# A decoder layer on one core: key tiles of 128, 128 and 16, and the order of attention and convolution work set by a VectorE budget

## The chip, the cores and the metric

The kernel runs on 1 core of one Trainium2 chip. The metric is the device time of one execution in microseconds (us); lower is better. The engines that matter here are TensorE (PE in the profile; PEld is its weight load), VectorE (DVE), ScalarE (ACT), GpSimd (POOL) and the queue that starts the weight transfers (SP).

## The reference, cut to what matters

One layer of a hybrid decoder, in float32: 16 meta tokens and 256 tokens (272 in all), model width 2048. One input projection feeds three groups of heads: 6 forgetting-attention heads ("fox"), 4 differential-attention heads ("diff") and a convolution module of 768 channels. Their outputs are joined, projected by `w_out`, added to the residual, and followed by a gated feed-forward part of width 5632.

```
h = rmsnorm(x);  proj = h @ w_in
fox : s = (q k^T) * 128**-0.5 + c[query] - c[key], causal;  p = softmax(s);  y = p @ v      # c = cumsum(log f)
diff: p = softmax(q1 k1^T / 8) - lam * softmax(q2 k2^T / 8), causal;  y = rmsnorm(p @ v) * 0.8
conv: u = a * sigmoid(g);  u = causal_dwconv31(u) + b;  y = silu(layernorm(u))
h = h + rmsnorm(concat(fox, diff, conv) @ w_out)
f = (silu(causal_dwconv3(h' @ w_gate)) * (h' @ w_up)) @ w_down        # h' = rmsnorm(h)
out = (h + rmsnorm(f))[16:]
```

The queries come in blocks: the 16 meta tokens, then 128 and 128 real tokens. A block sees all keys up to its own end. The kernel computes only the last two meta rows (258 query columns, `NQ`), since the later width-3 convolution needs no more of them.

## The kernel before, in words

Activations are kept transposed (features on partitions, tokens in the free dimension). Every projection multiplies a weight tile of 128x128 with 258 or 272 token columns. To keep float32 accuracy, both operands are cut into a high and a low part in fp32r, and `mm3` (L278 to L281) issues three matmuls: high by high, high by low, low by high. A weight chunk arrives by DMA on the SP queue (`load`), ScalarE makes its high part (L203), VectorE its low part (L204); `chunk()` does this one chunk ahead of its use.

**The input projection** runs in groups of up to four weight tiles (`in_groups`, `TOGETHER`); the text writes g4c2 for chunk 2 of group 4. Each chunk holds four k steps; after the fourth chunk `evac` copies the finished tiles out of PSUM. Group 1 and groups 4 and 5 give the convolution's inputs, groups 0, 2 and 3 the diff heads' q, k and v, groups 6 to 10 the fox heads'.

**Attention and convolution are laid between these matmuls by hand.** Each head is a Python generator (`fox`, L544; `diff`, L566). At a `yield` it stops until it is pumped again. In every chunk the first three heads that are waiting are pumped one stage each, after 8, 12 and 16 of the chunk's (tile, k) steps (L659). A fox head has the stages: scores and softmax; (empty); transposes of the probabilities (`probsT`); output. A diff head: scores and two softmaxes; their combination; (empty); transposes; output; (empty); normalised output. Behind the heads `pump_conv` (L256) issues convolution taps (L448, 31 taps for each of 6 channel tiles, 186 in all, VectorE) until a budget is spent: 2.1 or 1.9 a chunk, with 0.66 charged for two taps, 5.0 in group 10. When the taps are done, the same queue holds `layernorm` (L452), which goes through four stops: the sum over channel tiles; a matmul with ones (L459), subtractions and squares; the reciprocal root through TensorE, VectorE and GpSimd (`token_rstd`, L130, L120, L121); its spread over the partitions (L141) and the six results y10 to y15 (L478, L479, L486, L487). A bare `yield` there ends that pump.

**The output projection** (L685 to L714) works on four tiles at a time over 16 k steps in the order `KORD`: chunk 0 needs the diff heads' results y6 to y9, chunk 1 the fox heads' y0 to y3, chunk 2 y10 to y13 of the convolution, chunk 3 y14, y15, y4 and y5. Before each chunk of its first group the waiting heads and `pump_conv(4.0)` are pumped once (L688). The four PSUM banks of a group are held until its last chunk is done.

The compiler that turns the program into one instruction list for each engine keeps this order, except that an instruction whose inputs it takes to be late lets later ones go first.

**One head's tiles.** Keys are taken as 0 to 127 with only the first 16 counted (`vm`, scaled by a vector that is zero from 16 on), 16 to 143 and 144 to 271. `scores` (L508) makes 144 columns for the first block of queries, 272 for the second and 16 for the meta rows. `probsT` (L528) transposes six 128x128 pieces on TensorE into two PSUM banks; one VectorE copy (L538) and three ScalarE copies bring them back. The output takes three matmuls in a fox head (258, 256 and 128 columns) and six of 128 columns in a diff head. A float32 matmul is issued as two passes; a transpose is one. The masks are built by VectorE and GpSimd at the start (L103 to L112).

Of the kernel before, what the change touches and what calls it, by code (L numbers as in the profile page):

```python
# [9 lines left out]
F32 = mybir.dt.float32  # L10
# [7 lines left out]
P = 128  # L18
# [53 lines left out]
def hymba_kernel(ctx, tc, ins, out):  # L72
# [15 lines left out]
    def planes(n):  # L88
# [12 lines left out]
    mhalf = const.tile([P, 4], F32, name="mhalf")  # L101
# [15 lines left out]
    def rsqrt(out_t, in_t, n, d, eps, w):  # L117
        v = const.tile([P, 4], F32, name=f"var{cnt[0]}", tag="var", bufs=4)
# [213 lines left out]
    r0 = const.tile([P, 4], F32, name="r0")  # L332
    R0 = const.tile([P, T], F32, name="R0")
    r0f = const.tile([P, 4], F32, name="r0f")
    r0d = const.tile([P, 4], F32, name="r0d")
    r0m = const.tile([P, 1], F32, name="r0m")
    nc.vector.memset(r0m, 0.0)
# [33 lines left out]
    wf = const.tile([P, KT, FOXH], F32, name="wf")  # L371
# [65 lines left out]
    def conv(i):  # L437

        acc[i] = slot("C", NQ)
        for n, k in enumerate(range(CW - 1, -1, -1)):  # L440
# [8 lines left out]
            if n % 2:  # L449
                yield 0.66  # L450
# [42 lines left out]
    def values(vT, key):  # L493
        ps = bank()
        nc.tensor.transpose(out=ps[:, 0:P], in_=vT[:, 0:P], identity=ident)
        nc.tensor.transpose(out=ps[:, P:2 * P], in_=vT[:, NM:NM + P], identity=ident)
        nc.tensor.transpose(out=ps[:, 2 * P:3 * P], in_=vT[:, NM + P:T], identity=ident)
        v, vm = slot("T", 2 * P), slot("T", P)
        nc.scalar.mul(out=vm, in_=ps[:, 0:P], mul=r0m)
        nc.scalar.mul(out=v[:, 0:P], in_=ps[:, P:2 * P], mul=r0[:, 0:1])  # L500
        nc.scalar.mul(out=v[:, P:2 * P], in_=ps[:, 2 * P:3 * P], mul=r0[:, 1:2])
        return vm, v[:, 0:P], v[:, P:2 * P]

    def scores(maps):
# [3 lines left out]
        for o, n, a in ((0, 144, 2), (144, T, 130), (416, NM, 0)):  # L508
# [4 lines left out]
    def softmax_rows(ps, biasA, biasB, biasM, rs, key):  # L513

        pA, pB = slot("T", 160), slot("T", T)
        segs = ((pA[:, NM:160], ps[:, 0:144], biasA, P, 0), (pB, ps[:, 144:416], biasB, P, 1), (pA[:, 0:NM], ps[:, 416:432], biasM, P, 2))
# [9 lines left out]
        return [(pA[:, NM:160], P, 0), (pB, P, 1), (pA[:, 0:NM], P, 2)], pA, sm  # L526

    def probsT(pr, pA, key):  # L528
        pa, pb, pm = (x[0] for x in pr)
        tA, tB = bank(), bank()  # L530
        nc.tensor.transpose(out=tA[:, 0:P], in_=pa[:, 0:P], identity=ident)
        nc.tensor.transpose(out=tA[:, P:2 * P], in_=pb[:, 0:P], identity=ident)
        nc.tensor.transpose(out=tA[:, 2 * P:3 * P], in_=pa[:, 16:144], identity=ident)
        nc.tensor.transpose(out=tA[:, 3 * P:4 * P], in_=pb[:, 16:144], identity=ident)
        nc.tensor.transpose(out=tB[:, 0:P], in_=pb[:, 144:272], identity=ident)
        nc.tensor.transpose(out=tB[:, P:2 * P], in_=pA[:, 0:P], identity=ident)
        ptm, pta, ptb = slot("T", NQ), slot("T", 2 * P), slot("T", P)
# [443 lines left out]
```

## Time and profile before

| | |
|---|---|
| three runs | 1157.0, 1156.12, 1155.02 us; median 1156.12 |
| profiled execution | 1155.95 us, of which the span is 1154.1 us |
| PE busy | 1143.1 us (99%), 7768 matmuls |
| DVE busy | 765.4 us (66%) |
| ACT busy | 580.2 us (50%) |
| POOL busy | 69.4 us (6%) |
| granted TensorE clock | 0.998 of full speed |

Busy times are shares of the span. Matmuls overlap in their pipeline, so a matmul's own duration (some 0.28 us for 258 columns) is longer than the distance from its start to the next start (0.12 us); the distance is what it costs. VectorE's share is a mean over stages that differ: it is full in most of the input projection and at about half in the feed-forward part.

### The profile page before, as it was taken

What the parts mean: (1) busy time and instruction counts of PE and PEld (TensorE: products, weight loads), DVE (VectorE), ACT (ScalarE), POOL (GpSimd) and SP (SyncE); (2) the same over time, 40 slices, a digit from 0 to 9 for tenths busy, and PEclk for the clock granted to TensorE, in tenths of its full rate; (3) what the DMA queues carried; (4) which work ended last, traced back from release to release, by engine and by line L of the source; (5) the groups of instructions that cost most, each with busy time, mean ns of one, the idle gap of its engine ahead of it and who ended that gap; (6) DMA issues with size and microseconds to landing.
All of it is one profiled execution on the core that took longest, in us unless ns stands there. A gap on an engine that the chain in (4) does not pass through costs nothing.

```text
span 1154.1 us, 19333 instructions
## 1 busy us (share of the span) xinstructions
PE 1143.1 (99%) x7768; PEld 1059.2 (92%) x7768; DVE 765.4 (66%) x1298; ACT 580.2 (50%) x998; POOL 69.4 (6%) x120
## 2 busy tenths in 40 slices
PE   9999999999999999999999999999999999999997
PEld 8999999999999999999999999999999888888885
DVE  7699899985647589656766576567666645444544
ACT  8445764555856546544544454445445434343432
POOL 0010000001200038100000000000000100000001
PEclk9999999999999999999999999999999999999999
DMA  8555335333757437555555555555455755555554
GB/s 319 205 165 198 134 124 183 146 129 122 263 183 249 153 126 231 193 183 183 183 183 185 185 181 187 183 185 191 178 191 187 229 182 185 195 196 190 182 184 145
DMA packets 36522, 213.39 MB, mean 185 GB/s; under 512 B 5338, under 2 KB 8032, under 8 KB 12880
## 3 DMA queue, kind: packets, MB, share of 16 engines
q1 hardware_dynamic: 32400, 205.33, 49.6%
q0 software_dynamic: 3600, 6.29, 2.2%
q8 instruction: 61, 1.00, 0.3%
q10 hardware_dynamic: 432, 0.53, 0.2%
q14 instruction: 29, 0.24, 0.1%
HBM read 207.93 MB, written 4.20 MB: 184 GB/s over the span
## 4 chain that ended last, share of the span: by engine, by line
PE 97%; DMA 2%; DVE 1%; ACT 0%; issue 0%; SPq 0%; DVEq 0%; ACTq 0%
PE m L279 16%; PE m L280 16%; PE m L281 16%; PE m L774 13%; PE m L775 7%; PE m L854 4%; PE a L854 4%; PE m L856 4%; PE a L856 4%; PE a L855 4%; PE m L855 4%; DMA raw<-in_w_in 1%; PE a L774 1%; PE a L510 1%; PE a L281 1%; PE a L775 0%
## 5 line engine op out<-in xcount | busy, mean ns | idle before, releaser
L204 DVE TENSOR_TENSOR lo<-raw,hi 128x1024 fp32r<-128x1024 f32 (+2 forms) x382 | 452.0, 1202 | 320.6 <-ACT hi L203 319.4
L203 ACT CAST hi<-raw 128x1024 fp32r<-128x1024 f32 (+2 forms) x382 | 384.9, 1033 | 359.7 <-PE m L280 142.4
L279 PE MATMUL m<-R,hi 128*128 128x258 f32 (+1 forms) x1296 | 371.7, 288 | 1.1 <-ACT R L736 0.7
L280 PE MATMUL m<-R,hi 128*128 128x258 f32 (+1 forms) x1296 | 369.7, 286 | 0.0
L281 PE MATMUL m<-R,lo 128*128 128x258 f32 (+1 forms) x1296 | 368.0, 285 | 0.0
L279 PEld LDWEIGHTS m<-R,hi 128*128 128x128 f32 x1296 | 243.8, 189 | 3.2 <-ACT R L736 1.0
L280 PEld LDWEIGHTS m<-R,hi 128*128 128x128 f32 x1296 | 245.9, 190 | 0.3 <-DVE R L298 0.2
L281 PEld LDWEIGHTS m<-R,lo 128*128 128x128 f32 x1296 | 245.6, 190 | 0.0
L774 PE MATMUL m<-R,hi 128*128 128x512 f32 x656 | 231.2, 396 | 0.0
L775 PE MATMUL m<-R,lo 128*128 128x256 f32 x656 | 183.7, 280 | 0.0
L774 PEld LDWEIGHTS m<-R,hi 128*128 128x128 f32 x656 | 123.2, 188 | 27.9
L775 PEld LDWEIGHTS m<-R,lo 128*128 128x128 f32 x656 | 125.4, 191 | 0.0
L448 DVE SCALAR_TENSOR_TENSOR C<-C,vec,C 128x258 f32<-128x258 f32 (+12 forms) x180 | 80.6, 475 | 1.5
L279 PE MATMUL m<-Y,hi 128*128 128x258 f32 x256 | 72.9, 285 | 0.0
L280 PE MATMUL m<-Y,hi 128*128 128x258 f32 x256 | 72.6, 284 | 0.0
L281 PE MATMUL m<-Y,lo 128*128 128x258 f32 x256 | 72.0, 282 | 0.0
L280 PEld LDWEIGHTS m<-Y,hi 128*128 128x128 f32 x256 | 48.9, 191 | 0.0
L281 PEld LDWEIGHTS m<-Y,lo 128*128 128x128 f32 x256 | 48.8, 191 | 0.0
L279 PEld LDWEIGHTS m<-Y,hi 128*128 128x128 f32 x256 | 48.3, 189 | 0.0
L754 POOL DMA_DIRECT2D h1d<-K x64 | 37.1, 586 | 35.1 <-DVE K L752 29.8
L843 POOL DMA_DIRECT2D X<-in_gpost x8 | 4.4, 545 | 438.2 <-DVE T L796 427.5
L856 PE MATMUL m<-hi,Y 128*128 128x512 f32 x64 | 25.3, 395 | 0.0
(399 smaller groups left out, 1428.6 us busy)
## 6 DMA issues: line engine op xcount, KB each, us to landing
raw<-in_w_gate SPq DMA_DIRECT2D x44, 1024.0 KB, 4.8
raw<-in_w_down SPq DMA_DIRECT2D x44, 1024.0 KB, 4.8
raw<-in_w_up SPq DMA_DIRECT2D x41, 1024.0 KB, 4.8
raw<-in_w_in SPq DMA_DIRECT2D x37, 1024.0 KB, 4.8
raw<-in_w_out SPq DMA_DIRECT2D x16, 1024.0 KB, 5.1
raw<-in_w_in SPq DMA_DIRECT2D x8, 512.0 KB, 4.9
raw<-in_w_up SPq DMA_DIRECT2D x4, 768.0 KB, 4.2
X<-in_xT SPq DMA_DIRECT2D x16, 136.0 KB, 5.7
```

The costliest lines, as they stand in the source:

```text
L203: i = nc.scalar.copy(out=hi, in_=r)
L204: j = nc.vector.tensor_tensor(out=lo, in0=r, in1=hi.bitcast(F32), op=ALU.subtract)
L279: nc.tensor.matmul(out=ps, lhsT=wh, rhs=xh, start=first, stop=False)
L280: nc.tensor.matmul(out=ps, lhsT=wh, rhs=xl, start=False, stop=False)
L281: nc.tensor.matmul(out=ps, lhsT=wl, rhs=xh, start=False, stop=last)
L448: nc.vector.scalar_tensor_tensor(out=acc[i][:, j:NQ], in0=src, scalar=w, in1=acc[i][:, j:NQ], op0=ALU.mult, op1=ALU.add)
L754: nc.gpsimd.dma_start(out=place[j, i], in_=hs[32 * i:32 * i + 32, :].rearrange("a (q b) -> a q b", b=32))
L774: nc.tensor.matmul(out=both, lhsT=wh, rhs=hb[k][:, :, 2:NQ], start=k == 0, stop=False, skip_group_check=True)
L775: nc.tensor.matmul(out=ps[ti][:, 0:SEQ], lhsT=wl, rhs=hh[k][:, 2:NQ], start=False, stop=k == KT - 1, skip_group_check=True)
L854: nc.tensor.matmul(out=po[n][t], lhsT=ah[k][:, s], rhs=wh, start=k == 0, stop=False)
L855: nc.tensor.matmul(out=po[n][t], lhsT=ah[k][:, s], rhs=wl, start=False, stop=False)
L856: nc.tensor.matmul(out=po[n][t], lhsT=al[k][:, s], rhs=wh, start=False, stop=k == FT - 1)
```

## The change

The keys are taken as 0 to 127, 128 to 255 and 256 to 271 (all of the first tile counts). The score blocks get 160, 272 and 32 columns, the further ones masked, so that 32x32 squares line up. `probsT` makes three TensorE transposes into one bank; the three corners that these leave out are turned by VectorE in 32x32 squares. The targets `p0`, `e1`, `e2` are three standing sets whose unused parts `prepare` sets to zero once. A fox head's output takes 258, 144 and 16 columns. The values' tiles are scaled by the reciprocal roots of tokens 0, 128 and 144 on (`r0e` is zero below row 112), for which `stats0` computes a fifth window.

Masks are no longer built at the start but by GpSimd in `prepare`, called in g3c0. `wf` moves to a rotating buffer, and `R0` and `R2s` share one.

The empty stages go. Each `yield` now tells what the next stage costs; `pick` takes the waiting heads, in order, that fit a budget of 3.5 a chunk (less a charge for the copies of a chunk 3; the first is always taken), and the rest of the budget, at least 0.8, goes to convolution taps, two for 0.8. `CB` and its 5.0 in group 10 go.

```diff
-    mask = const.tile([P, 416], F32, name="mask")
-    nc.vector.memset(mask, 0.0)
-    nc.gpsimd.affine_select(out=mask[:, 0:144], in_=mask[:, 0:144], pattern=[[-1, 144]], base=NM,
-                            channel_multiplier=1, compare_op=ALU.is_ge, fill=NEG)
-    nc.gpsimd.affine_select(out=mask[:, 144:416], in_=mask[:, 144:416], pattern=[[-1, 272]], base=NM + P,
-                            channel_multiplier=1, compare_op=ALU.is_ge, fill=NEG)
-    maskm = const.tile([P, NM], F32, name="maskm")
-    nc.vector.memset(maskm, 0.0)
-    nc.gpsimd.affine_select(out=maskm, in_=maskm, pattern=[[-1, NM]], base=Q0,
-                            channel_multiplier=1, compare_op=ALU.is_ge, fill=NEG)
+    from112 = const.tile([P, 1], F32, name="from112")
+    nc.gpsimd.affine_select(out=from112, in_=ones[:, 0:1], pattern=[[0, 1]], base=-112, channel_multiplier=1, compare_op=ALU.is_ge, fill=0.0)
...
+    ahead = {}
+
     def pump_job(j):
         try:
-            next(j)
+            ahead[j] = next(j) or 0.0
         except StopIteration:
             heads.remove(j)
+
+    def pick(budget):
+
+        jobs = []
+        for j in list(heads)[:3]:
+            c = ahead.get(j, 1.0)
+            if c <= budget or not jobs:
+                jobs.append(j)
+                budget -= c
+        return jobs, budget
...
-        spread0 = token_rstd([ssx], float(D), EPS, (NM, NM + P, 0, Q0), ((2, 0, NM, 0), (0, 0, P, NM), (1, 0, P, NM + P)), r0, True, "m")
+        spread0 = token_rstd([ssx], float(D), EPS, (NM, NM + P, 0, Q0, P), ((2, 0, NM, 0), (0, 0, P, NM), (1, 0, P, NM + P)), r0, True, "m")
         yield
         ps = spread0(True)
         nc.scalar.copy(out=R0, in_=ps[:, 0:T])
-        nc.vector.tensor_copy(out=r0m[0:NM], in_=r0[0:NM, 2:3])
-        nc.vector.tensor_scalar(out=r0f, in0=r0, scalar1=FOXS, scalar2=None, op0=ALU.mult)
-        nc.vector.tensor_scalar(out=r0d, in0=r0, scalar1=DIFFS, scalar2=None, op0=ALU.mult)
+        nc.vector.tensor_tensor(out=r0e, in0=r0[:, 1:2], in1=from112, op=ALU.mult)
...
-                yield 0.66
+                yield 0.8
...
+    mask, sets, nset = [], [], [0]
+
+    def prepare():
+
+
+        ma, mb = slot("X", 192), slot("X", T)
+        for t, o, n, base in ((ma, 0, 160, NM), (ma, 160, 32, Q0), (mb, 0, T, NM + P)):
+            x = t[:, o:o + n]
+            nc.gpsimd.memset(x, 0.0)
+            nc.gpsimd.affine_select(out=x, in_=x, pattern=[[-1, n]], base=base, channel_multiplier=1, compare_op=ALU.is_ge, fill=NEG)
+        mask.extend([ma[:, 0:160], mb, ma[:, 160:192]])
+        for _ in range(3):
+            p0, e1, e2 = slot("X", NQ), slot("X", 256), slot("X", P)
+            for x in (p0[:, 0:2], e1[:, 0:P], e2):
+                nc.gpsimd.memset(x, 0.0)
+            sets.append((p0, e1, e2))
...
+        for i, (o, r) in enumerate(((0, r0[:, 2:3]), (P, r0[:, 4:5]), (NM + P, r0e))):
+            nc.tensor.transpose(out=ps[:, i * P:(i + 1) * P], in_=vT[:, o:o + P], identity=ident)
+            nc.scalar.mul(out=v[i], in_=ps[:, i * P:(i + 1) * P], mul=r)
+        return v
...
-        for o, n, a in ((0, 144, 2), (144, T, 130), (416, NM, 0)):
+        for o, n, a in ((0, 160, 2), (160, T, 130), (432, 32, 0)):
...
-    def probsT(pr, pA, key):
-        pa, pb, pm = (x[0] for x in pr)
-        tA, tB = bank(), bank()
-        nc.tensor.transpose(out=tA[:, 0:P], in_=pa[:, 0:P], identity=ident)
-        nc.tensor.transpose(out=tA[:, P:2 * P], in_=pb[:, 0:P], identity=ident)
-        nc.tensor.transpose(out=tA[:, 2 * P:3 * P], in_=pa[:, 16:144], identity=ident)
-        nc.tensor.transpose(out=tA[:, 3 * P:4 * P], in_=pb[:, 16:144], identity=ident)
-        nc.tensor.transpose(out=tB[:, 0:P], in_=pb[:, 144:272], identity=ident)
-        nc.tensor.transpose(out=tB[:, P:2 * P], in_=pA[:, 0:P], identity=ident)
-        ptm, pta, ptb = slot("T", NQ), slot("T", 2 * P), slot("T", P)
-        nc.vector.tensor_copy(out=ptm[:, 0:2], in_=tB[:, P:P + 2])
-        nc.scalar.copy(out=ptm[:, 2:NQ], in_=tA[:, 0:2 * P])
-        nc.scalar.copy(out=pta, in_=tA[:, 2 * P:4 * P])
-        nc.scalar.copy(out=ptb, in_=tB[:, 0:P])
-        return ptm, pta, ptb
+        return [(pA[:, 32:192], P, 0), (pB, P, 1), (pA[:, 0:32], P, 2)], (pA, pB), sm
+
+    def probsT(p):
+
+
+        pA, pB = p
+        p0, e1, e2 = sets[nset[0] % 3]
+        nset[0] += 1
+        ps = bank()
+        for i, x in enumerate((pA[:, 32:160], pB[:, 0:P], pB[:, P:256])):
+            nc.tensor.transpose(out=ps[:, i * P:(i + 1) * P], in_=x, identity=ident)
+        nc.vector.transpose(out=p0[0:32, 0:32], in_=pA[0:32, 0:32])
+        nc.vector.transpose(out=e1[0:32, 96:P], in_=pA[96:P, 160:192])
+        nc.vector.transpose(out=e2[96:P, 96:P], in_=pB[96:P, 240:T])
+        nc.scalar.copy(out=p0[:, 2:NQ], in_=ps[:, 0:256])
+        nc.scalar.copy(out=e1[:, P:256], in_=ps[:, 256:384])
+        return p0, e1, e2
...
             nc.scalar.mul(out=x, in_=x, mul=r[0:n, c:c + 1])
-        yield
-        if h < FOXH - 1:
-            yield
-        ptm, pta, ptb = probsT(p, pA, key)
-        yield
+        yield 0.6
+        p0, e1, e2 = probsT(pt)
+        yield 0.4
         o = bank()
-        nc.tensor.matmul(out=o[:, 0:NQ], lhsT=vm, rhs=ptm, start=True, stop=False)
-        nc.tensor.matmul(out=o[:, 2:NQ], lhsT=va, rhs=pta, start=False, stop=False)
-        nc.tensor.matmul(out=o[:, 130:NQ], lhsT=vb, rhs=ptb, start=False, stop=True)
+        nc.tensor.matmul(out=o[:, 0:NQ], lhsT=v[0], rhs=p0, start=True, stop=False)
+        nc.tensor.matmul(out=o[:, 114:NQ], lhsT=v[1], rhs=e1[:, 112:256], start=False, stop=False)
+        nc.tensor.matmul(out=o[:, 242:NQ], lhsT=v[2], rhs=e2[:, 112:P], start=False, stop=True)
...
     def diff(h, qT, kT, vT):
...
-        yield
+        yield 1.1
...
-        yield
-        yield
-        ptm, pta, ptb = probsT(p1, pA, key)
-        yield
+        yield 0.6
+        p0, e1, e2 = probsT(pt)
+        yield 0.2
...
-        yield
-        yield
+        yield 0.0
+        yield 0.4
...
-            heads.append(diff(i, q, k, v) if d else fox(i, q, k, v))
-
-    CB = {9: 2.1, 10: 5.0}
+            j = diff(i, q, k, v) if d else fox(i, q, k, v)
+            ahead[j] = 3.6 if d else 2.8
+            heads.append(j)
...
-                jobs = list(heads)[:3]
+                jobs, left = pick(3.5 - (sum(dict(k=0.4, a=0.6, g=0.6).get(x[0][-1], 0.0) for x in g) if c == 3 else 0.0))
...
                     lam()
+                    prepare()
...
-                    pump_conv(CB.get(gi, 2.1 if gi < 4 else 1.9))
+                    pump_conv(max(left, 0.8))
```

## Rows read from the trace of the kernel before

**Rows 1.** The page of the profile: busy us of each engine, share, instructions
```profile
PE 1143.1 (99%) x7768; PEld 1059.2 (92%) x7768; DVE 765.4 (66%) x1298; ACT 580.2 (50%) x998; POOL 69.4 (6%) x120
```

**Rows 2.** Waits of PE: engine, line, released by, us in total, times, longest
```profile
PE m L279 <- DVE C L431: 0.3, 1, 0.3
```

**Rows 3.** Windows: stretch, its length, busy PE, PEld, DVE, ACT, POOL (instructions), clock, DMA
```profile
108.00:140.00 32.00, 32.00 (x267) 31.20 (x266) 25.20 (x75) 25.37 (x76) 0.00 (x0) 1.00 0.39 141
...
246.00:279.00 33.00, 33.00 (x261) 32.57 (x260) 16.44 (x38) 17.97 (x47) 0.00 (x0) 1.00 0.25 90
279.00:294.60 15.60, 15.60 (x126) 15.35 (x125) 14.17 (x36) 12.71 (x31) 5.17 (x7) 1.00 0.78 277
```

**Rows 4.** Timeline of PE, one head's transposes: start, us, engine, line, operation
```profile
210.81 0.27 PE L531 MATMUL a<-ident,T 128*128 128x128 f32 x1
...
211.35 0.27 PE L536 MATMUL a<-ident,T 128*128 128x128 f32 x1
```

**Rows 5.** Timeline of PE, one fox head's output
```profile
217.36 0.60 PE L561 MATMUL a<-T,T 128*128 128x258 f32 x2
217.80 0.59 PE L562 MATMUL a<-T,T 128*128 128x256 f32 x2
218.23 0.38 PE L563 MATMUL a<-T,T 128*128 128x128 f32 x2
```

**Rows 6.** Timeline of PE, one fox head's scores (first rows, last pass, next matmul)
```profile
199.28 0.41 PE L510 MATMUL a<-Q,Q 128*128 128x144 f32 x2
...
200.01 0.26 PE L510 MATMUL a<-Q,Q 128*128 128x16 f32 x1
200.12 0.36 PE L279 MATMUL m<-R,hi 128*128 128x258 f32 x1
```

**Rows 7.** Timeline of all engines, the layer norm's steps
```profile
278.05 0.60 PE L459 MATMUL a<-C,ones 128*128 128x258 f32 x2
...
286.33 0.80 PE L130 MATMUL a<-ones,C 128*128 128x1 f32 x6
...
287.98 1.89 POOL L121 TENSOR_TENSOR rt<-var,mhalf 128x3 f32<-128x3 f32 x1
...
289.95 0.80 PE L141 MATMUL a<-ident,rt 128*128 128x128 f32 x6
...
290.90 2.08 DVE L478 TENSOR_TENSOR C<-C,a 128x258 f32<-128x258 f32 x6
...
291.40 1.05 ACT L203 CAST hi<-raw 128x1024 fp32r<-128x1024 f32 x1
292.47 1.28 ACT L479 ACT_TABLE_LOAD   x1
...
293.76 1.10 ACT L479 ACTIVATE C<-C,vec 128x258 f32<-128x258 f32 x2
...
297.60 0.43 DVE L487 TENSOR_TENSOR Y<-C,Y 128x258 fp32r<-128x258 f32 x1 [0.37 <-ACT Y L486]
```

**Rows 8.** Timeline of ACT: a table load whose activation waits for VectorE
```profile
64.20 1.28 ACT L360 ACT_TABLE_LOAD   x1
68.23 0.20 ACT L360 ACTIVATE lamex<-lamsm 128x2 f32<-128x2 f32 x1 [2.75 <-DVE lamsm L358]
```

**Rows 9.** Timeline of PE, the output projection's start and fox head 5's scores in it
```profile
294.63 0.37 PE L279 MATMUL m<-Y,hi 128*128 128x258 f32 x1
...
299.52 0.27 PE L495 MATMUL a<-ident,Q 128*128 128x128 f32 x1
...
300.69 0.36 PE L281 MATMUL m<-Y,lo 128*128 128x258 f32 x1
```

**Rows 10.** One line's instructions: the small VectorE copy (ns least, median, most)
```profile
L538 DVE COPY T<-a x10: 148/155/160, 133.4 to 309.6; 128x2 f32<-128x2 f32 x10
```

**Rows 11.** Windows at the end of the span, columns as in rows 3
```profile
1145.30:1149.90 4.60, 0.17 (x1) 0.00 (x0) 3.73 (x9) 1.68 (x6) 1.96 (x3) 1.00 0.48 161
1149.90:1154.00 4.10, 0.00 (x0) 0.00 (x0) 0.04 (x1) 0.00 (x0) 0.00 (x0) 0.50 0.52 165
```

More of the change, by code (lines that the diff above doesn't have):

```diff
@@ L117, in rsqrt @@
     def rsqrt(out_t, in_t, n, d, eps, w):
-        v = const.tile([P, 4], F32, name=f"var{cnt[0]}", tag="var", bufs=4)
+        v = const.tile([P, 5], F32, name=f"var{cnt[0]}", tag="var", bufs=4)
         cnt[0] += 1
@@ L330, in hymba_kernel @@
     nc.vector.tensor_scalar(out=gs, in0=vec[:, V_GSUB:V_GSUB + 1], scalar1=1.0 - LAM_INIT, scalar2=None, op0=ALU.mult)
-    r0 = const.tile([P, 4], F32, name="r0")
-    R0 = const.tile([P, T], F32, name="R0")
+    r0 = const.tile([P, 5], F32, name="r0")
+    R0 = const.tile([P, T], F32, name="R0", tag="spread")
     r0f = const.tile([P, 4], F32, name="r0f")
     r0d = const.tile([P, 4], F32, name="r0d")
-    r0m = const.tile([P, 1], F32, name="r0m")
-    nc.vector.memset(r0m, 0.0)
+    r0e = const.tile([P, 1], F32, name="r0e")
     def stats0():
-        spread0 = token_rstd([ssx], float(D), EPS, (NM, NM + P, 0, Q0), ((2, 0, NM, 0), (0, 0, P, NM), (1, 0, P, NM + P)), r0, True, "m")
+        spread0 = token_rstd([ssx], float(D), EPS, (NM, NM + P, 0, Q0, P), ((2, 0, NM, 0), (0, 0, P, NM), (1, 0, P, NM + P)), r0, True, "m")
         yield
@@ L369, in hymba_kernel @@
     ckb, cqA, cqM = [], const.tile([P, 2, 6], F32, name="cqA"), const.tile([P, 6], F32, name="cqM")
-    wf = const.tile([P, KT, FOXH], F32, name="wf")
+    wf = slot("T", KT * FOXH).rearrange("p (k h) -> p k h", h=FOXH)
     nc.gpsimd.dma_start(out=wf, in_=ins["w_f"])
@@ L490, in put_y, with values @@
             nc.vector.scalar_tensor_tensor(out=yl[k], in0=src, scalar=scale, in1=yh[k].bitcast(F32), op0=ALU.mult, op1=ALU.subtract)
-    def values(vT, key):
-        ps = bank()
[L495 to L502, printed above, removed]
+    mask, sets, nset = [], [], [0]
[11 more added lines that the diff above has]
+            sets.append((p0, e1, e2))
+    def values(vT):
+        ps = bank()
+        v = slot("T", 2 * P), slot("T", P)
+        v = v[0][:, 0:P], v[0][:, P:2 * P], v[1]
+        for i, (o, r) in enumerate(((0, r0[:, 2:3]), (P, r0[:, 4:5]), (NM + P, r0e))):
+            nc.tensor.transpose(out=ps[:, i * P:(i + 1) * P], in_=vT[:, o:o + P], identity=ident)
+            nc.scalar.mul(out=v[i], in_=ps[:, i * P:(i + 1) * P], mul=r)
+        return v
     def scores(maps):
         pss = [bank() for _ in maps]
-        for o, n, a in ((0, 144, 2), (144, T, 130), (416, NM, 0)):
+        for o, n, a in ((0, 160, 2), (160, T, 130), (432, 32, 0)):
             for ps, (qT, kT) in zip(pss, maps):
@@ L544, in fox @@
     def fox(h, qT, kT, vT):
         key = f"f{h}"
-        vm, va, vb = values(vT, key)
-        biA, biB = slot("T", 144), slot("T", T)
-        biasm = wk.tile([P, NM], F32, tag="biasm", name=f"biasm{h}")
-        nc.vector.scalar_tensor_tensor(out=biA, in0=mask[:, 0:144], scalar=cqA[:, 0, h:h + 1], in1=ckb[h][:, 0:144], op0=ALU.add, op1=ALU.subtract)
-        nc.vector.scalar_tensor_tensor(out=biB, in0=mask[:, 144:416], scalar=cqA[:, 1, h:h + 1], in1=ckb[h], op0=ALU.add, op1=ALU.subtract)
-        nc.vector.scalar_tensor_tensor(out=biasm, in0=maskm, scalar=cqM[:, h:h + 1], in1=ckb[h][:, 0:NM], op0=ALU.add, op1=ALU.subtract)
@@ L552, in fox @@
-        p, pA, r = softmax_rows(scores([(qT, kT)])[0], biA, biB, biasm, r0f, key)
+        v = values(vT)
+        bi, biB = slot("T", 192), slot("T", T)
+        nc.vector.scalar_tensor_tensor(out=bi[:, 0:160], in0=mask[0], scalar=cqA[:, 0, h:h + 1], in1=ckb[h][:, 0:160], op0=ALU.add, op1=ALU.subtract)
+        nc.vector.scalar_tensor_tensor(out=biB, in0=mask[1], scalar=cqA[:, 1, h:h + 1], in1=ckb[h], op0=ALU.add, op1=ALU.subtract)
+        nc.vector.scalar_tensor_tensor(out=bi[:, 160:192], in0=mask[2], scalar=cqM[:, h:h + 1], in1=ckb[h][:, 0:32], op0=ALU.add, op1=ALU.subtract)
@@ L576, in diff @@
             nc.vector.scalar_tensor_tensor(out=x, in0=y, scalar=rb[0:n, c:c + 1], in1=x, op0=ALU.mult, op1=ALU.add)
-        yield
-        yield
-        ptm, pta, ptb = probsT(p1, pA, key)
-        yield
+        yield 0.6
+        p0, e1, e2 = probsT(pt)
+        yield 0.2
         o = bank()
-        nc.tensor.matmul(out=o[:, 0:P], lhsT=ptm[:, 2:130], rhs=vm, start=True, stop=False)
-        nc.tensor.matmul(out=o[:, 0:P], lhsT=pta[:, 0:P], rhs=va, start=False, stop=True)
-        nc.tensor.matmul(out=o[:, P:2 * P], lhsT=ptm[:, 130:258], rhs=vm, start=True, stop=False)
-        nc.tensor.matmul(out=o[:, P:2 * P], lhsT=pta[:, P:2 * P], rhs=va, start=False, stop=False)
-        nc.tensor.matmul(out=o[:, P:2 * P], lhsT=ptb, rhs=vb, start=False, stop=True)
-        nc.tensor.matmul(out=o[:, 2 * P:3 * P], lhsT=ptm[:, 0:P], rhs=vm, start=True, stop=True)
+        nc.tensor.matmul(out=o[:, 0:P], lhsT=p0[:, 2:130], rhs=v[0], start=True, stop=False)
+        nc.tensor.matmul(out=o[:, 0:P], lhsT=e1[:, 0:P], rhs=v[1], start=False, stop=True)
+        nc.tensor.matmul(out=o[:, P:2 * P], lhsT=p0[:, 130:258], rhs=v[0], start=True, stop=False)
+        nc.tensor.matmul(out=o[:, P:2 * P], lhsT=e1[:, P:256], rhs=v[1], start=False, stop=False)
+        nc.tensor.matmul(out=o[:, P:2 * P], lhsT=e2, rhs=v[2], start=False, stop=True)
+        nc.tensor.matmul(out=o[:, 2 * P:3 * P], lhsT=p0[:, 0:P], rhs=v[0], start=True, stop=True)
         ss = wk.tile([P, 3], F32, tag="ss", name=f"ss{h}")
@@ L729, in hymba_kernel @@
     h1d = dpool.tile([SEQ, D], F32, name="h1d")
-    R2s = const.tile([P, NQ], F32, name="R2s")
+    R2s = const.tile([P, NQ], F32, name="R2s", tag="spread")
     def h1(j):
```

16 lines of the change are left out of this document (9 added, 7 removed).

## The prediction, made before the change was run

> **What bounds the kernel now.** I read the page's busy times first. TensorE is busy 99% of the span, VectorE 66%, ScalarE 50% [rows 1]. The waits of TensorE come next: of four waits in the whole span one lies among the attention work, 0.3 us for VectorE's gate copies [rows 2]. So the kernel takes what TensorE's instruction stream takes, and a change pays by taking instructions out of that stream or costs by putting a hole into it. The windows tell where VectorE could make such a hole. It is nearly full until 246 us except in 108 to 140 (25.2 of 32.0 us, three diff heads at once), and half empty in 246 to 279 (16.4 of 33.0) [rows 3]: the taps are done early. The timeline of TensorE gives prices, always as the distance between starts.
>
> **TensorE's work.** (a) Transposes. Six of one head start from 210.81 to 211.35, 0.108 us apart [rows 4]. Three fewer in each of 10 heads: 30 x 0.108 = 3.2 us. (b) A fox head's output. The 256-column matmul takes two passes, 217.80 to 218.23, 0.215 each [rows 5]; with 144 columns a pass is like one of the scores, two of which end 0.41 us after the first starts against 0.29 for one alone, 0.12 apart [rows 6]. 6 heads x 2 x 0.09 = 1.1 us. Its last matmul goes from 128 to 16 columns; a 16-column pass still holds TensorE from 200.01 to 200.12 [rows 6], as a 128-column one does, so 0. (c) Scores of 160 and 32 columns. A 144-column pass costs 0.012 us more than a transpose's 128 columns, so 16 more cost about that: 2 passes x 10 heads (a diff head's two maps go side by side) = 0.2 us lost. 32 columns cost as much as 16. (d) The fifth window in `stats0` is two more one-column passes; six such take 286.33 to 286.99 [rows 7], so 0.2 us lost. A diff head's output keeps six matmuls. Sum of (a) to (d): 3.2 + 1.1 - 0.2 - 0.2 = 3.9 us saved. Bounds: 3.2 if 144 columns save a third less and the wider scores cost double, 5.2 if the 12 passes of 16 columns cost nothing after all (12 x 0.11 more).
>
> The Trainium skill speaks of (a) too: "TensorE: Matmul & The Clock Gate", Part 4, puts a transpose at about 275 ns in a kernel. By that the 30 would give 8.3 us and the sum 8.9. The trace agrees with 0.27 as a duration but starts six in 0.54 us [rows 4], so they overlap and the rule gets next to no chance.
>
> **Costs at nothing, and their cover.** VectorE gets three 32x32 turns for each head in place of one small copy of 0.155 us [rows 10]; I take 0.155 for each (0.15 to 0.43, a full 258-column operation [rows 7]): 20 x 0.155 = 3.1 us (up to 8). ScalarE loses one copy a head. Neither engine is on the path while it is ahead of TensorE. GpSimd builds masks and zeros in g3c0; the first user is D0's softmax, four chunks of some 6 us later. At the start the masks were built beside the first transfers, so taking them away gives 0. The wait of [rows 2] came from D3's softmax standing before the gate copies; there the combination of D1 stands now, and I take the 0.3 us back (0 to 0.5).
>
> **The moved step that is not hidden.** I counted where the code puts the taps and the layer norm. Before: 33 taps in g2, 29 in g3, then 6, 24, 25, 25, 25 and the last 19 in g9, done in g9c2. The ones-matmul follows in g9c3, the reciprocal root after g10c1, spread and y10 to y15 after g10c2. That is three chunks ahead of their use in chunk 2 of the output projection. After: budget 3.5 gives ten taps a chunk where no head is waiting (35 in g2, 27 in g3), but a diff head's first stage takes it all (3.6), and heads now come one after another, so later groups get 4, 22, 35, 17, 17, 16, 13. The last three taps fall in g10c2. There `layernorm` does its sum and stops; in g10c3 come the ones-matmul and five of six subtractions; before chunk 0 of the output projection the sixth, and a stop; before chunk 1 the reciprocal root, and a stop; before chunk 2 the spread L141 and y10 to y15, which that chunk needs at once. TensorE has nothing else then: the four banks are held, and the chunk's first tile needs y10, y11, y12 and y13 in turn. Behind the waiting matmul stand the rest of chunk 2, chunk 3 and all that follows.
>
> The price, from the spread's first matmul (t = 0; 289.95 in [rows 7]): the six take 0.66; the chunk could pass its first three k steps in 3 x 3 x 0.12 = 1.1 (40 matmuls from 294.63 to 299.52 [rows 9]) and would want y13 at t = 1.8. The multiplications L478 start at t = 0.95 and the first ends at 1.4. From the first silu (293.76) to the end of y13's low part (297.60 + 0.43) are 4.3 us, paced by ScalarE at 0.8 us a tile. If the silu follows the first multiplication, y13 is there at 5.7 and TensorE loses 3.9 us. In the rows before, a split of 1.05 and a table load of 1.28 stood ahead of the silu, which began only at t = 3.8: loss 6.2. A table load does not wait for its activation's data (64.20 against 68.23) [rows 8], but it does stand behind what ScalarE has in hand; the split of the next chunk becomes possible just when chunk 1 frees its buffers, at t = 0. One split and the load from t = 0.1: silu at 2.4, loss 4.9. I take 4.9, between the ends 3.9 and 6.2, because [rows 7] show just this pair ahead of the silu. Bound from below: 1 us less if fox head 5's transposes and output are still open and fill the hole.
>
> **Sum.** Profiled execution 1155.95 - 3.9 - 0.3 + 4.9 = 1156.65; this execution stands 0.2 below the median of the three runs (1156.12), too little to correct for. I give 1156.6: what the transposes give, the layer norm takes.
>
> **Rivals.** *Faster: no hole.* If the spread gets ahead of chunk 1's matmuls in TensorE's list, or the layer norm is done early, only the savings stay: 1155.95 - 3.9 - 0.3 = 1151.8. For it: the order is not strictly that of the code, fox head 5's scores stand after 40 of chunk 0's 48 matmuls [rows 9]. Against: that move is backward, of an instruction whose inputs were late; L130 and L141 stand where the code puts them or later. Chance 0.32.
>
> *Slower: VectorE is late with the last taps.* From 246 to 294.6 it idles 48.6 - 30.6 = 18.0 us [rows 3]. The change brings two diff heads from 108-140 into the later stretch: 25.2 us of that window is three heads and splits, so between 5 and 16.8, I take 9; and 3.1 to 8 us of turns. 18.0 - 9 - 3.1 leaves 6 us, at the other end -7. The layer norm has slack: from the ones-matmul to the spread it took 11.9 us (278.05 to 289.95) [rows 7], while now two chunks (11.6), head 5's scores (1.2) [rows 9] and some 1.6 of its own and head 5's passes lie between, 14.4. Once the sum over channels comes over 2.5 us late, each further us is lost: 7 - 2.5 = 4.5 us, 1156.65 + 4.5 = 1161.2. For it: VectorE had no idle time where the taps now thin out. Against: the middle values. Chance 0.18.
>
> *Slower still: the clock falls in the hole.* The granted clock is 1.00 (2.4 GHz) in all of the work and 0.50 (1.2 GHz) in the last window, after TensorE had ended [rows 11]. An estimate: at half speed chunk 2's 48 matmuls (0.12 each) take 5.8 us more, 1162.4. The Trainium skill, same page, "HAM oscillation", says that idle gaps between bursts bring this. Against: the hole comes in pieces, 2 to 3 us and then under 1, with matmuls between. Chance 0.04.
>
> *The change does not do what it says:* if the short passes hold TensorE as the long ones did, only the transposes pay, 1.1 us less: 1157.8. This lies in the forecast's range.
>
> **How the numbers follow.** Chances: forecast 0.46, faster rival 0.32, slower two 0.22. The forecast's own range is 1153.2 to 1159.0 (hole 2.9 to 6.2, savings 3.2 to 5.2, wait 0 to 0.5). The whole range takes in most of the faster case and the start of the slower: 1151.4 to 1160.0. A change of under 0.2% (2.3 us) counts as none: faster 0.33 (the rival and a little of the forecast's low end), same 0.43, slower 0.24 (the two rivals and the forecast's high end).
>
> **What would show it.** In the profile after: 30 fewer transposes of the probabilities, 0.108 us apart; L141 of the layer norm after the first 96 matmuls of the output projection; behind it a wait of TensorE on ScalarE's or VectorE's y10 to y13 of 4 to 6 us in pieces; ScalarE at that moment with split, table load, silu. The forecast is wrong if that wait is missing or under 2.5 us, if waits on low parts of weights appear in g2 to g10, or if the ones-matmul comes later than g10's end.

## The result and the profile after

The changed kernel takes 1165.26 us (median of 4 runs, 1164.38 to 1166.31) against 1156.01 before (4 runs): ratio 1.008, 95% interval 1.0063 to 1.0098. It is slower by 9.3 us; the forecast said 1156.6 and its range ended at 1160.0.

From here on a kernel's difference is taken against the kernel before in its own series (medians 1156.01, 1156.63, 1156.32 and 1156.38 in the four). The profiled execution of the changed kernel took 1165.87 us, 9.9 more than the one before; its span is 10.1 us longer (1164.2 after 1154.1). Three stretches of TensorE's time divide that, beside a start 0.2 us shorter: from its `stats0` matmuls at about 51 us to the first matmul of the output projection +1.9 (245.56 after 243.68, although most of the savings lie here and the layer norm's last passes have left it), the output projection +8.0 (103.38 after 95.40), and all behind it +0.4. Busy times have hardly moved [rows 1]:

```profile
span 1164.2 us, 19323 instructions
...
PE 1147.4 (99%) x7740; PEld 1058.9 (91%) x7740; DVE 770.0 (66%) x1315; ACT 577.7 (50%) x986; POOL 71.0 (6%) x133
```

The list has 28 matmuls fewer (30 transposes less, two passes more in `stats0`), and TensorE is busy 4 us longer. What it waits for tells more. Waits of PE after (us in total, times, longest), against the one wait of [rows 2]:

```profile
PE m L283 <- ACT Y L489: 2.7, 1, 2.7
...
PE a L519 <- ACT T L520: 2.7, 2, 1.7
...
PE m L284 <- DVE Y L490: 0.5, 1, 0.5
```

Waits of its weight load, same columns:

```profile
PEld a L519 <- ACT T L520: 6.5, 13, 2.1
```

Two places then: Y is the convolution's result (the layer norm), and L519 and L520 are the transposes of the values and ScalarE's copies of them. The weight load's list shows the second place 13 times where PE's own list shows it twice.

**The savings came as forecast.** Timeline of PE after, one head's transposes and one fox head's output (start, us, engine, line):

```profile
206.06 0.49 PE L555 MATMUL a<-ident,T 128*128 128x128 f32 x3
...
222.64 0.60 PE L577 MATMUL a<-X,T 128*128 128x258 f32 x2
223.07 0.41 PE L578 MATMUL a<-X,T 128*128 128x144 f32 x2
223.32 0.29 PE L579 MATMUL a<-X,T 128*128 128x16 f32 x2
```

Three transposes end 0.49 us after the first starts, so their starts lie 0.11 apart as in [rows 4]. The two passes of 144 columns take 0.25 us from start to start, where 256 took 0.43 [rows 5].

**The layer norm's hole.** Timeline of all engines after, answering [rows 7] (lines in the order of time):

```profile
296.08 0.60 PE L462 MATMUL a<-C,ones 128*128 128x258 f32 x2
...
308.17 0.73 PE L122 MATMUL a<-ones,C 128*128 128x1 f32 x6
...
310.23 1.99 ACT L195 CAST hi<-raw 128x1024 fp32r<-128x1024 f32 x2
...
311.70 0.81 PE L133 MATMUL a<-ident,rt 128*128 128x128 f32 x6
...
312.13 0.36 ACT L489 CAST Y<-a 128x258 fp32r<-128x258 f32 x1
...
312.51 1.28 ACT L482 ACT_TABLE_LOAD   x1
...
313.81 1.09 ACT L482 ACTIVATE C<-C,vec 128x258 f32<-128x258 f32 x2
...
315.25 0.75 PE L283 MATMUL m<-Y,hi 128*128 128x258 f32 x4 [2.74 <-ACT Y L489]
...
316.10 0.39 ACT L489 CAST Y<-C 128x258 fp32r<-128x258 f32 x1
```

The ones-matmul comes at the end of group 10, the spread after 96 matmuls of the output projection, and ahead of the silu stand a split, a cast of a fox head's result and the table load. The silu begins 2.1 us after the spread; the forecast had 2.4. Four matmuls by a high part (L283) go in a row from 315.25 on, and the next high part is cast only from 316.10: they are all four tiles' steps with y10, which the compiler has let go ahead of the first tile's steps with y11 to y13.

Windows after, from the spread on (stretch, length, busy PE, PEld, DVE, ACT, POOL with counts, granted clock, DMA share, GB/s):

```profile
311.70:315.20 3.50, 0.81 (x9) 0.72 (x7) 3.49 (x9) 3.47 (x7) 0.00 (x0) 1.00 0.50 137
315.20:318.90 3.70, 3.14 (x15) 2.94 (x16) 2.87 (x7) 3.52 (x9) 1.65 (x4) 0.59 0.63 234
318.90:322.60 3.70, 3.70 (x19) 3.70 (x19) 0.33 (x1) 0.00 (x0) 3.65 (x7) 0.50 0.75 221
322.60:326.30 3.70, 3.70 (x32) 3.70 (x31) 1.23 (x2) 2.00 (x2) 0.00 (x0) 0.99 0.27 79
```

After the wait of 2.74 us four matmuls still run at the full clock (the last three start 0.12 us apart); from 316.5 on the granted clock is at the lower level (0.50, 1.2 GHz) until 322.6, and after that back at 2.4 GHz. In between 28 matmuls start 0.214 us apart, not 0.12: 28 x 0.095 = 2.7 us. So the 8.0 us of the output projection are 1.25 of layer-norm passes that lay before it until now (six one-column passes and the spread), 2.7 of clock and some 4.0 that are left, nearly all of it the hole: 3.0 up to the first matmul and some 0.8 up to y10's low part. The rule of the Trainium skill that the prediction weighed ("TensorE: Matmul & The Clock Gate", "HAM oscillation": idle gaps between bursts bring the lower clock) held here, behind a wait of 2.74 us.

**The values.** Timeline after, PE, its weight load and ScalarE, at the start of diff head 1:

```profile
150.84 0.27 PE L519 MATMUL a<-ident,Q 128*128 128x128 f32 x1
...
151.04 0.54 PE L529 MATMUL a<-Q,Q 64*128 64x160 f32 x4
...
151.15 0.37 ACT L520 ACTIVATE T<-a,r 128x128 f32<-128x128 f32 x1 [2.00 <-PE a L519]
151.57 0.14 PEld L519 LDWEIGHTS a<-ident,Q 128*128 128x128 f32 x1 [0.23 <-ACT T L520]
...
151.83 0.72 PE L529 MATMUL a<-Q,Q 64*128 64x272 f32 x2
151.94 0.37 ACT L520 ACTIVATE T<-a,r 128x128 f32<-128x128 f32 x1 [0.42 <-PE a L519]
...
152.48 0.14 PEld L519 LDWEIGHTS a<-ident,Q 128*128 128x128 f32 x1 [0.36 <-ACT T L520]
...
153.54 0.39 PE L283 MATMUL m<-R,hi 128*128 128x272 f32 x1
```

The changed `values` issues transpose, copy, transpose, copy, transpose, copy, all in one PSUM tile. Each transpose waits for ScalarE's copy of the piece before (the copy ends at 151.52, the next transpose's weights load at 151.57), although it writes another part of the tile; a few scores fill the time. From first transpose to next projection matmul: 2.70 us.

### The profile page after: what moved, and what is told of

It is laid out like the page before. It is cut to its first block, busy times and chain, and to the rows that moved or that the text cites. A ratio compares the mean times of both kernels' runs of the same rounds, so it can differ in the third digit from the quotient of the medians.

```text
span 1164.2 us, 19323 instructions
## 1 busy us (share of the span) xinstructions
PE 1147.4 (99%) x7740; PEld 1058.9 (91%) x7740; DVE 770.0 (66%) x1315; ACT 577.7 (50%) x986; POOL 71.0 (6%) x133
## 4 chain that ended last, share of the span: by engine, by line
PE 88%; DVE 8%; issue 1%; ACT 1%; DMA 0%; POOL 0%; DVEq 0%; SPq 0%; ACTq 0%; POOLq 0%
PE m L284 14%; PE m L283 14%; PE m L285 14%; PE m L791 13%; PE m L792 7%; PE a L871 4%; PE a L873 4%; PE m L871 4%; PE m L873 4%; PE m L872 4%; PE a L872 4%; DVE C L451 3%; DVE lo L196 2%; PE a L791 1%; PE a L285 1%
## 5 line engine op out<-in xcount | busy, mean ns | idle before, releaser
L283 PE MATMUL m<-R,hi 128*128 128x258 f32 (+1 forms) x1296 | 371.2, 288 | 0.8 <-ACT R L753 0.7
L283 PEld LDWEIGHTS m<-R,hi 128*128 128x128 f32 x1296 | 243.6, 188 | 2.7 <-ACT R L753 1.0
L451 DVE SCALAR_TENSOR_TENSOR C<-C,vec,C 128x258 f32<-128x258 f32 (+13 forms) x180 | 80.6, 475 | 1.1
L283 PE MATMUL m<-Y,hi 128*128 128x258 f32 x256 | 73.7, 290 | 2.7 <-ACT Y L489 2.7
L283 PEld LDWEIGHTS m<-Y,hi 128*128 128x128 f32 x256 | 49.5, 194 | 2.9 <-ACT Y L489 2.8
L284 PEld LDWEIGHTS m<-Y,hi 128*128 128x128 f32 x256 | 50.1, 196 | 0.7 <-DVE Y L490 0.7
```

The source lines that it names most:

```text
L283: nc.tensor.matmul(out=ps, lhsT=wh, rhs=xh, start=first, stop=False)
L284: nc.tensor.matmul(out=ps, lhsT=wh, rhs=xl, start=False, stop=False)
L451: nc.vector.scalar_tensor_tensor(out=acc[i][:, j:NQ], in0=src, scalar=w, in1=acc[i][:, j:NQ], op0=ALU.mult, op1=ALU.add)
```

## The experiments

Theory at the start: the loss has three parts, the values in turns, the late layer norm with its clock, and something in the new stage order. Line numbers in the diffs are left out.

**The values' order mended.**

```diff
-        for i, (o, r) in enumerate(((0, r0[:, 2:3]), (P, r0[:, 4:5]), (NM + P, r0e))):
+        for i, o in enumerate((0, P, NM + P)):
             nc.tensor.transpose(...)
+        for i, r in enumerate((r0[:, 2:3], r0[:, 4:5], r0e)):
             nc.scalar.mul(...)
```

> The kernel after, with one edit: the three transposes of a head's values are issued first and the three ScalarE copies behind them, as before the change. Theory A (in the input projection TensorE waits for ScalarE, because each of the three transposes now stands behind the copy that reads the one before it; the trace of after shows 7.1 us more in the lines of scores and values): 1165.3 - 7.1 = 1158.2 us, between 1157 and 1160, the waits of TensorE on L520 gone. Rival B (the waits come from the new order of the heads and a full VectorE or ScalarE; the loop in values is innocent): 1164 to 1166.

1161.13 us (5 runs), +4.5 against before: 4.7 less than the changed kernel. The same head in its timeline of PE:

```profile
151.17 0.49 PE L519 MATMUL a<-ident,Q 128*128 128x128 f32 x3
151.59 1.14 PE L530 MATMUL a<-Q,Q 64*128 64x160 f32 x12
152.67 0.39 PE L283 MATMUL m<-R,hi 128*128 128x272 f32 x1
```

1.50 us in place of 2.70. Over all ten heads the scores and values take 6.7 us less of TensorE by starts, of which the median shows 4.7; small waits for ScalarE's splits and query copies (0.6 and 0.8 us) come up elsewhere.

**The layer norm early.**

```diff
-                    pump_conv(max(left, 0.8))
+                    pump_conv(max(left, {8: 1.9, 9: 2.1, 10: 5.0}.get(gi, 0.8)))
```

> The kernel after, with one edit: in groups 8, 9 and 10 the convolution budget is at least 1.9, 2.1 and 5.0, so that the layer norm's steps stand where they stood before the change (spread and y10 to y15 after chunk 2 of group 10). Theory A (the hole in chunk 2 of the output projection is made by the late spread, and the lower clock behind it by the hole: 3.8 us of waiting and 28 matmuls at 0.214 in place of 0.120 us, 2.7 us): 1165.3 - 6.5 = 1158.8 us, between 1157.5 and 1160, granted clock 1.00 from 294 to 400 us. Rival B (VectorE is too full in groups 8 to 10, so taps put earlier only make the waits appear there): under 2 us gained, 1163.3 or more, with waits of TensorE on low parts of weights or on the gate copies.

1161.96 us, +5.3. The output projection is back at 95.22 us, without hole and at full clock, but the stretch before it grew by 3.7, of which 1.25 are the layer norm's passes. That is dearer than expected; with the values mended as well the same edit costs 2.2 there (next run). The trace shows where the other 1.5 went. A transpose of the values waits for ScalarE, and behind it the clock falls; the same wait in the changed kernel's profile (1.67 us, at 238.48) is followed by the full clock. The wait, then the windows behind it, of this run and of the changed kernel:

```profile
238.92 0.33 PE L519 MATMUL a<-ident,Q 128*128 128x128 f32 x1 [1.69 <-ACT T L520]
```

```profile
239.30:242.70 3.40, 3.40 (x18) 3.34 (x19) 3.38 (x13) 1.76 (x7) 0.00 (x0) 0.50 0.63 263
```

```profile
238.80:242.20 3.40, 3.40 (x30) 3.36 (x30) 3.39 (x12) 1.71 (x7) 0.00 (x0) 1.00 0.65 270
```

The 3.4 us hold 18 matmuls here and 30 there; the 12 missing ones are worth some 12 x 0.12 = 1.4 us. Four of this run's five executions, the profiled one among them, have a mean granted clock of 0.996, lower than any of the kernel before (0.997 to 0.999); the fifth, with 0.998, took 1159.88 us, 2.1 less than the median. So the values in turns can cost clock as well as waits.

**Both.**

> Both edits of the two runs before on the kernel after. Theory A (two separate losses, 7.1 and 6.5 us, and 3.9 us of TensorE work saved as forecast): 1165.3 - 13.6 = 1151.7 us, between 1151 and 1153, 0.3 to 0.4% below the kernel before. Rival B (the losses are one, a stage order that leaves an engine full, and moving either only shifts it): 1156 or more.

1155.85 us (11 runs), -0.8, ratio 0.9993 (0.9984 to 1.0002). Between this run and the first lies the late layer norm alone: 4.5 + 0.8 = 5.3 us. It was not the 1151.7 expected: something of 3 us was left.

**Key tiles alone.** Values mended; the old empty stages, three heads a chunk and old tap budgets put back.

```diff
-        yield 0.6
-        p0, e1, e2 = probsT(pt)
-        yield 0.4
+        yield
+        if h < FOXH - 1:
+            yield
+        p0, e1, e2 = probsT(pt)
+        yield
...
-                jobs, left = pick(3.5 - ...)
+                jobs = list(heads)[:3]
...
-                    pump_conv(max(left, 0.8))
+                    pump_conv({9: 2.1, 10: 5.0}.get(gi, 2.1 if gi < 4 else 1.9))
```

> The key tiles of 128, 128 and 16 alone: the new tiles, transposes and corners with the values' transposes issued first, but stages, empty yields and tap budgets as before the change. The forecast's sum of TensorE work (3.2 + 1.1 - 0.2 - 0.2 = 3.9 us saved): 1156.0 - 3.9 = 1152.1 us, between 1151.3 and 1153. Rival B (the corners on VectorE or the wider scores cost what the transposes give): 1155 or more.

1153.06 us (6 runs), -3.6, ratio 0.997 (0.9959 to 0.9982): the fastest version here, ahead of both kernels. In its waits of PE only the gate copies are left in the attention work:

```profile
PE m L283 <- DVE C L434: 0.5, 1, 0.5
```

**The values in turns, in the kernel before.**

```diff
         nc.tensor.transpose(out=ps[:, 0:P], ...)
+        nc.scalar.mul(out=vm, ...)
         nc.tensor.transpose(out=ps[:, P:2 * P], ...)
+        nc.scalar.mul(out=v[:, 0:P], ...)
         nc.tensor.transpose(out=ps[:, 2 * P:3 * P], ...)
-        nc.scalar.mul(out=vm, ...)
-        nc.scalar.mul(out=v[:, 0:P], ...)
         nc.scalar.mul(out=v[:, P:2 * P], ...)
```

> The kernel before, with one edit: each of the three transposes of a head's values is followed at once by the ScalarE copy that reads it. Theory A (the order in that loop by itself makes TensorE wait for ScalarE; in the kernel after the scores' and values' lines took 7.1 us more in all, most of it in the four diff heads): 1156.6 + 6 = 1162.6 us, between 1160 and 1165, with waits of TensorE on the values' copies. Rival B (it needs the new stage order, where heads come one at a time): under 2 us slower.

1159.72 us (8 runs), +3.4, ratio 1.0027 (1.0017 to 1.0037). The order alone costs, though less than in the changed kernel. Waits of its weight load:

```profile
PEld a L498 <- ACT T L497: 1.9, 8, 0.4
...
PEld a L500 <- ACT T L499: 0.7, 2, 0.4
```

**The hole filled.** 26 idle bf16 matmuls ahead of chunk 2 in the changed kernel.

```diff
+            if g == 0 and c == 2:
+                busy(26)
             order = [(ti, kk) for ti in range(4) for kk in range(4)]
```

> The kernel after, with one edit: 26 matmuls of 128x256 bf16 on constants (0.11 us each, 2.9 us in all) stand ahead of chunk 2 of the output projection, where TensorE waits for y10. Theory A (the wait of about 3.8 us lets the granted clock fall, and the 28 matmuls at half speed cost 2.7 us by themselves): the wait stays, now filled, the granted clock stays 1.00, 1165.3 - 2.7 = 1162.6 us, between 1161.8 and 1163.5. Rival B (the clock has another cause, or the filling delays what TensorE waits for): 1165 or more, with a granted clock of 0.50 behind the hole as before.

1165.05 us, +8.7. In its profile the clock is 1.00 throughout and the output projection takes 100.67 us, 2.7 less, but the start of that execution (to `stats0`) was 1.5 us longer, and the medians give only 0.5. The profiled execution has a mean granted clock of 0.998; the other four have 0.996 three times and 0.997 once. No execution of the kernel before has less than 0.997, so in three of them the clock most likely fell somewhere. Their values come in turns, as in the run with the layer norm early, where the clock fell behind such a wait, but no trace shows where it fell in these. Inconclusive by time; the pair of runs with the late layer norm in the kernel before, below, fills the hole without the values in turns.

**A PSUM bank for each of the values' transposes.**

```diff
-        ps = bank()
...
         for i, (o, r) in enumerate(...):
+            ps = bank()
-            nc.tensor.transpose(out=ps[:, i * P:(i + 1) * P], ...)
+            nc.tensor.transpose(out=ps[:, 0:P], ...)
```

> The kernel after, with one edit: each of the three transposes of a head's values writes a PSUM bank of its own; the order transpose, copy, transpose, copy stays. Theory A1 (a transpose waits for the copy before it because both touch the same PSUM tile): the waits of TensorE on L520 go, and with the 4.1 us that the first run gained: 1165.3 - 4 = 1161.3 us. Theory A2 (the wait comes from the order in ScalarE's queue, not from the shared tile): the waits stay, 1164 or more. More banks in use may cost some us of their own in waits for a free one.

1164.36 us, +8.0, so little of the expected gain. The waits on L520 are gone, which shows that the shared tile causes them; waits for a free bank take their place, and behind the longer of them the granted clock is 0.50 from 231.7 to 235.0:

```profile
PE a L529 <- DVE Y L493: 2.3, 1, 2.3
...
PE a L529 <- ACT T L613: 1.0, 1, 1.0
```

The Trainium skill ("PSUM — Partial Sum Buffer", "PSUM bank collisions raise a hardware error") says that two engines must keep out of one bank in the same partitions, even at different addresses, and that the compiler adds a dependency to keep them apart. The traces agree: with one bank 6.5 us of waits in 13 rows, with three banks none of that kind.

**The combination stage behind the copies of a group's last chunk** (both mended besides).

```diff
+                late = [j for j in jobs if c == 3 and gi > 3 and ahead[j] > 0.6]
+                jobs = [j for j in jobs if j not in late]
...
                         evac(kind, i, pss[gi][ti])
+                for j in late:
+                    pump_job(j)
```

> The third run's kernel (values' transposes first, layer norm early), with one edit: in a group's last chunk the stages of heads that cost over 0.6 (a diff head's combination in groups 5 and 8) are issued behind the copies that free the group's PSUM banks, not ahead of them. Theory A (what is left of the loss against the old stages, 155.85 to 153.06 above a thousand, is in part TensorE waiting at the change of groups, 0.9 and 1.1 us in the trace of the third run, for copies that stand behind three ScalarE multiplications): 1155.85 - 1.5 = 1154.3 us, and the two waits under 0.4 us each. Rival B (the copies are late for another reason): within 0.5 us of 1155.85.

1155.59 us (11 runs), -0.7: the same as without it. In its profile the wait of 0.8 us for a group's copies shrank to 0.4, but a wait of 1.0 us of the transposes of the probabilities for ScalarE's scaling came up. Moving the copies does not bring the 3 us back.

**The late layer norm in the kernel before.**

```diff
-        yield
+        for _ in range(5):
+            yield
         ps = bank()
...
             yield 0.75
         yield
+        yield
         rb = token_rstd([s], 768.0, EPS, *NQ_TOK)
```

> The kernel before, with its layer norm alone held back by empty stops, so that the spread over the partitions and y10 to y15 come right before chunk 2 of the output projection, as in the changed kernel. Nothing of the tiles, heads or taps changes. Theory A: the late layer norm costs what the output projection of the changed kernel shows, a hole of about 4.3 us and 2.7 us of half clock behind it: 1156.3 + 7.0 = 1163.3. Theory B: the hole alone is general and the fall of the clock belongs to the changed kernel's own pattern of stops: 1160.6, with the granted clock at 1.00 behind the hole. Theory C: most of what the changed kernel lost there has other reasons: below 1159.

1161.58 us (5 runs), +5.2, ratio 1.0047 (1.0034 to 1.0059). Between A and B, and equal to the 5.3 of the other pair, so the late layer norm costs this in either kernel. PE waits 3.13 us for L488. Its windows from the end of the spread (columns as above):

```profile
309.60:312.70 3.10, 0.03 (x1) 0.00 (x0) 3.10 (x8) 2.56 (x5) 0.00 (x0) 1.00 0.64 217
312.70:316.60 3.90, 3.77 (x16) 3.53 (x17) 2.52 (x7) 3.52 (x10) 2.21 (x4) 0.58 0.56 176
316.60:320.00 3.40, 3.40 (x30) 3.40 (x29) 0.11 (x1) 0.10 (x1) 3.17 (x6) 0.98 0.70 205
```

**And filled,** with the edit of the filled hole.

> The run with the held-back layer norm in the kernel before, and 26 idle TensorE matmuls laid into the hole ahead of chunk 2. Theory A: the clock stays at 1.00 and the output projection is 2.7 us shorter than without them: 1160.6 where the run without comes to 1163.3. Rival: the filling matmuls cost about what the clock gives (they stand ahead of chunk 2 also where its tiles are there): within 0.5 us of the run without, with the clock at 1.00 in both or with the hole longer by what the clock gave.

1159.99 us (5 runs), +3.6: 1.6 less than unfilled, where the output projection of the two profiles differs by 1.8. Its windows:

```profile
310.00:315.00 5.00, 4.73 (x43) 4.15 (x42) 4.64 (x11) 4.45 (x10) 0.48 (x1) 1.00 0.58 210
315.00:320.00 5.00, 5.00 (x44) 5.00 (x43) 1.62 (x4) 3.14 (x8) 4.12 (x9) 1.00 0.58 161
```

So of 5.2 us the hole has 3.6 and the lower clock 1.6.

**No empty stages.** Key tiles alone, with the empty stages taken out again.

```diff
-        yield
-        if h < FOXH - 1:
-            yield
+        yield 0.6
         p0, e1, e2 = probsT(pt)
...
```

> The best version (key tiles alone, old stages, 1153.1) with one thing of the new stage order put back: the empty stages of the heads are gone, three heads a chunk as before, the old tap budgets. Theory A: what the new order costs beside the layer norm (2.8 us) comes from stages that follow each other with no chunk between, so that TensorE finds ScalarE's copies late: 1155 or more, with waits of TensorE on ScalarE among groups 2 to 10. Theory B: it comes from the budget, which lays diff heads one after another and moves the taps: within 0.7 of 1153.1.

1155.64 us (11 runs), -0.7, ratio 0.9992 (0.9983 to 1.0001): 2.8 us dearer than with them, which is theory A and all that was left over. Waits of PE, with the first of them in the timeline:

```profile
PE a L556 <- DVE T L593: 0.6, 1, 0.6
...
PE a L556 <- ACT T L573: 0.3, 1, 0.3
```

```profile
168.12 0.29 PE L285 MATMUL m<-R,lo 128*128 128x272 f32 x1
169.06 0.30 PE L556 MATMUL a<-ident,T 128*128 128x128 f32 x1 [0.65 <-DVE T L593]
```

L556 transposes the probabilities, L593 is VectorE's combination of a diff head's two maps and L573 ScalarE's scaling of a fox head's. With an empty stage between, both are done in time (PE has no such wait in key tiles alone); without it TensorE meets them late: from the projection matmul ahead to the transpose it is 0.94 us from start to start here, 0.59 at 207.0 and 0.32 twice, in place of 0.12, and the projection matmuls queued behind wait too. From `stats0` to the output projection this profile is 2.1 us longer than that of key tiles alone: by starts 1.4 in the projection matmuls, 0.5 in the fox outputs and 0.3 in the transposes.

**And heads picked by budget.**

```diff
-                jobs = list(heads)[:3]
+                jobs, left = pick(3.5 - ...)
```

> As the run without empty stages, and heads picked by the budget of 3.5 a chunk; taps still by the old fixed budgets, so the layer norm stays early. Theory A (empty stages): the same as the run without empty stages within 0.7. Theory B1 (the picking of heads): 1155 or more here, 1153 there. Theory B2 (the taps that take the rest of the budget): 1153.1 within 0.7 in both; the cost then comes only with the taps by budget, 1155.9.

1156.28 us (11 runs), -0.1: 0.6 above the run before it. That is inside the 0.7 that theory A allowed, but more than the scatter of the runs (the means of eleven runs each lie 0.60 apart, with a standard error of 0.19), so picking by itself may cost some 0.6. With taps by budget too, which is the run with both mended, it is -0.8: picking and budgeted taps together cost nothing that these runs can tell.

## Why the prediction was wrong

Differences to the kernel before, one edit after the other: key tiles alone -3.6; empty stages gone -0.7, so +2.8; picking and taps by budget -0.8, so 0; layer norm late +4.5, so +5.3; values in turns +9.3, so +4.7.

- **Savings (a) to (d), 3.9, and the wait of 0.3:** 3.6 measured. By starts on TensorE, key tiles alone against before: transposes 5.85 to 3.03, fox outputs 6.10 to 4.94, scores 9.20 to 9.52. The wait of [rows 2] did not come back as a gain: 0.5 there. Right in mechanism, 0.6 too much. The rival in which the short passes pay nothing is refuted by the fox outputs.
- **`values`, failed:** the diff shows the new loop, and the prediction has no term for it. It says only that "Neither engine is on the path while it is ahead of TensorE". Counting instructions, not their order, hid that three transposes had become three round trips to ScalarE: +4.7.
- **Empty stages, failed:** their going was used to count where taps fall, and priced at nothing. They were the time in which softmax, combination and copies got done: +2.8.
- **The moved layer norm, 4.9:** right in place, engines and order, and 5.3 in all, but as two terms: a hole of 3.6, below the bound of 3.9, and 1.6 of clock (2.7 in the changed kernel's profile). The hole was mis-sized at "the chunk's first tile needs y10, y11, y12 and y13 in turn": since the compiler laid the other tiles' steps ahead, TensorE lost the time up to y10 (2.74 us, then 0.5), not up to y13.
- **Rivals.** The clock's fall, given 0.04, came: its argument against, that the hole comes in pieces, failed on a first piece of 2.74 us. Its price of 5.8 for a whole chunk at half speed was too high; 28 of 48 matmuls ran so at most. VectorE late with the taps did not come: the ones-matmul stood at 296.08, at the end of group 10, and a 32x32 turn took 0.20 us. The faster rival, without a hole, did not come either.
- **Two sums** are off by their own rows, and nothing in the outcome hangs on them: the hole's upper end is 3.8 + 4.3 - 1.8 = 6.3, not 6.2, and thirty turns of 0.43 in place of ten copies of 0.155 would be 11 us, not 8.
- **The range** ended at 1160.0 because its bounds took in only the costed edits. Forecast and result lie 8.6 us apart in their differences: 4.7 + 2.8 + 0.6 + 0.4 = 8.5.

The values in turns cost 5.3 + 0.8 = 6.1 beside the early layer norm, where the clock falls behind their wait, 4.7 beside the hole and 3.4 in the kernel before. Open: how often it fell there in the executions without a trace, of the changed kernel and of the run with the filled hole, and so how the 4.7 divides into waits and clock; and why the kernel before loses only 3.4.

## What to carry to other kernels

Where TensorE is 99% busy, read a diff for the order of instructions between engines as well as for their number: producer and consumer issued in turns in one PSUM tile make every step a round trip, and the weight load's waits show it better than PE's own. A stage that does nothing may be what gives another engine its time; before it is taken out, look up when its successor's inputs are done. A hole in TensorE has two prices, its length and the slower matmuls that can follow it.

## What the runs showed of the hardware

- The clock was granted in full in the stretch with the wait of 2.74 us and was at 1.2 GHz from the fifth matmul behind it on. It fell behind a wait of 1.69 us in one profile and stayed at 2.4 GHz behind the same wait, 1.67 us, in another.
- What the clock costs differs between executions of one kernel: of the changed kernel's four, the two with a mean granted clock of 0.997 took 1164.38 and 1164.66 us, those with 0.995 and 0.994 took 1165.87 and 1166.31.
- 26 idle matmuls in the hole kept 2.4 GHz there in the profiles of both kernels; in the kernel before all five executions have a mean granted clock of 0.998.
- A transpose into one part of a PSUM tile waited for ScalarE's read of another part of it, 13 times, 6.5 us.
- The time from the start to `stats0` varies between the profiled executions of these kernels, from 50.75 to 52.36 us: a difference under 1.6 us between two profiles is not one of the edits until the stretches are compared.
